# Block 1's down-projection as seven products, weight differences made ahead through ScalarE's DMA queue, and the final norms moved into the up stages

## The chip, the cores and the metric

The kernel runs on one core of a Trainium2 chip. The metric is the device time in microseconds of one execution; the time of a kernel is the median of its runs. Engines are named as in the profile: PE is TensorE, PEld its weight loads, DVE VectorE, ACT ScalarE, POOL GpSimd, SP the engine whose queue issues most DMAs.

## The reference, cut to what matters

One layer of an encoder: attention and an mLSTM mix 2048 prompt rows and 128 sample rows, then comes the part that the change touches, a gated convolutional feed-forward network with a norm on both sides (D_MODEL 1024, D_FF 2816):

```python
def conv_ffn(h, buf, w_up, w_conv, b_conv, w_down):
    S = h.shape[1]
    u = h @ w_up
    ext = jnp.concatenate([buf.astype(u.dtype), u], axis=1)
    y = b_conv
    for j in range(CONV_W):
        y = y + ext[:, j:j + S] * w_conv[j]
    gate, up = jnp.split(y, 2, axis=-1)
    out = (jax.nn.gelu(gate, approximate=True) * up) @ w_down
    return out, ext[:, S:]
...
    ffn, new_buf = conv_ffn(rms_norm(x, norm_g[2]), conv_buf, w_up, w_conv, b_conv, w_down)
    x = x + rms_norm(ffn, norm_g[3])
```

`w_down` has 2816 rows and 1024 columns. All of it is float32.

## The kernel before

**Arithmetic.** Every product is taken in three passes (`mm3`, L93 to L97): each operand is split into a high part (a cast on ScalarE, L1265) and a low part (a subtraction on VectorE, L1266, the two are `split`), and L95 multiplies high by high, L96 and L97 high by low and low by high, all into one PSUM accumulator.

**Stages.** The first 1319 us hold the projections, attention, mLSTM and `project` (the output projection with the first residual, rows `x2d`). Then the feed-forward runs over three blocks of tiles of 128 rows, `FBLOCKS`: tiles 0 to 5, 6 to 11, and 12 to 15 with the sample tile. Each block has an up stage and a down stage.

The **up stage** loops over f, 22 slices of 128 of the 2816 inner columns. The slice's u is made of seven products of half-sized matrices (`product`, accumulators `ua`, `ub`, `uec`) with weight quads `wu` of 128x512; block 0 computes sums of the weights and stores them (`wsd`), blocks 1 and 2 load them. VectorE adds the products up (L1419, L1491, L1493, L1508), the convolution `y` takes ScalarE and VectorE (L1438 to L1442), the gated product g (L1514) goes to DRAM (`gd`) through GpSimd's queue. GpSimd also copies the halo columns (L1430, L1435).

The **down stage** multiplies g by `w_down`: two halves `dh` of 512 columns, each 22 k, six tiles and three passes into six accumulators (`dn`, `dnm`). `load_down` brings weights in chunks of four k (raw quads `wdr`, split into `wdh` and `wdl`, two buffers each), `fetch` brings g back from DRAM (`gr`), `split_g` splits it into `gh` and `gl` (four buffers `w3`). At a half's end VectorE copies the accumulators out (L1340), ScalarE squares them for the norm (L1344), and GpSimd's queue stores them (`f0d`, `f1d`).

**Interleaved work.** `h2_units(b + 1, ...)` prepares the next block's operand B (norm, transposes, sums, splits), a step after most k, and `later(t, rs)` finishes rows of the block before: it loads `f0d` or `f1d` and `x2d`, multiplies by the norm's factor on VectorE (L1376), adds the residual on GpSimd (L1377) and stores to the output (L1378). Before, these run in the down stages of blocks 1 and 2, between the units of `h2_units`. Raw rows live in a pool of eleven 2 KB buffers, `quad`.

**What sets the order.** The tile framework allocates buffers from pools, puts in the semaphore waits and orders each engine's instructions by a planned timeline; operations in `tc.keep_in_program_order` keep their place relative to the program. Each engine runs its own list in order, so a waiting instruction holds back all behind it on that engine. DMAs are issued from the list of the engine that names them (`nc.sync`, `nc.scalar`, `nc.gpsimd`).

## Time and profile before

| | us |
|---|---|
| runs | 2798.23, 2791.51, 2785.69 (median 2791.51) |
| profiled execution | 2788.08, its span 2786.4, granted clock 0.998 |
| block 0: up, down stage | 324.5, 195.9 |
| block 1: up, down stage | 318.2, 194.0 |
| block 2: up stage, down stage with the end | 268.4, 166.4 |

The stage lengths are read off the timeline at the first matmul of each stage (1319.0, 1643.5, 1839.4, 2157.6, 2351.6 and 2620.0 us from the span's start). A group's row in the profile reads: line, engine, operation, output<-inputs with shapes, count | busy us, mean ns of one | idle time of the engine just before them, and what ended it. A row of the timeline reads: start, length, engine, line, operation, count, and in brackets the idle time before it with its releaser.

### The profile page before, as it was taken

Reading aid. Unit: us, or ns where it says so; the run is one execution under the profiler, and the core shown is the slowest. Engines: PE = TensorE matmul, PEld = TensorE weight load, DVE = VectorE, ACT = ScalarE, POOL = GpSimd, SP = SyncE. Lnnn points to the kernel's source line nnn. Section 1 sums busy time; section 2 is a strip of 40 time slices with the busy share of each in tenths; the row PEclk is TensorE's granted clock in tenths of the full one; section 3 lists DMA queues with packets and bytes.
Section 4 is the critical chain, followed back from the end, with each engine's and each line's share of the span. In section 5 each row is a group of like instructions: output and inputs, shape, how many; then the busy total and the mean of one; then the engine's idle time right before and its main releaser. Section 6 shows DMA issues by size and latency. Waiting matters only on the chain.

```text
span 2786.4 us, 47181 instructions
## 1 busy us (share of the span) xinstructions
PE 2724.6 (98%) x16587; PEld 2549.6 (92%) x16587; DVE 1875.3 (67%) x3447; ACT 1407.9 (51%) x2836; POOL 555.4 (20%) x1095
## 2 busy tenths in 40 slices
PE   8999999999999999999999999999999999999998
PEld 7899999998899998888999988899999878999987
DVE  5344455656456667766999986457877864888855
ACT  4345455645356666533544555345555643555543
POOL 1000010211100002344533320011111421222330
PEclk9999999999999999999999999999999999999999
DMA  5544355557555455346645455644444774555585
GB/s 183 157 121 133 103 172 160 163 156 214 166 173 149 142 170 179 111 156 220 211 167 170 160 180 179 221 140 156 154 155 140 280 260 154 171 180 176 195 311 189
DMA packets 300171, 486.05 MB, mean 174 GB/s; under 512 B 55426, under 2 KB 150622, under 8 KB 299806
## 3 DMA queue, kind: packets, MB, share of 16 engines
q1 hardware_dynamic: 242334, 378.81, 43.9%
q0 software_dynamic: 19008, 70.40, 6.5%
q10 hardware_dynamic: 38592, 33.83, 3.6%
q8 instruction: 130, 2.13, 0.3%
q14 instruction: 107, 0.88, 0.1%
HBM read 359.36 MB, written 126.70 MB: 174 GB/s over the span
## 4 chain that ended last, share of the span: by engine, by line
PE 53%; DVE 3%; DMA 2%; issue 1%; POOL 1%; ACT 1%; SPq 0%; DVEq 0%; POOLq 0%; ACTq 0%
PE uec L95 6%; PE uec L96 6%; PE uec L97 6%; PE dn L97 4%; PE dn L96 4%; PE dn L95 4%; PE ua L97 3%; PE ua L96 3%; PE ua L95 3%; PE dnm L97 2%; PE dnm L95 2%; PE dnm L96 2%; PE ub L97 1%; PE ub L96 1%; PE ub L95 1%; PE wo L97 1%
## 5 line engine op out<-in xcount | busy, mean ns | idle before, releaser
L95 PE MATMUL uec<-B,wuh 128*128 128x384 f32 (+1 forms) x720 | 235.1, 328 | 3.1 <-DVE uu L1508 2.8
L96 PE MATMUL uec<-B,wuh 128*128 128x384 f32 (+1 forms) x720 | 235.1, 327 | 0.0
L97 PE MATMUL uec<-B,wul 128*128 128x384 f32 (+1 forms) x720 | 233.7, 327 | 0.0
L1266 DVE TENSOR_TENSOR gl<-gr,gh 128x768 fp32r<-128x768 f32 (+3 forms) x141 | 119.4, 856 | 153.1 <-ACT gh L1265 152.8
L1265 ACT CAST gh<-gr 128x768 fp32r<-128x768 f32 (+3 forms) x141 | 102.1, 736 | 210.3 <-PE dn L96 186.3
L1265 ACT CAST wuh<-wu 128x512 fp32r<-128x512 f32 x255 | 141.7, 618 | 110.4 <-PE uec L96 99.9
L95 PE MATMUL dn<-wdh,gh 128*128 128x512 f32 x466 | 182.7, 392 | 3.0 <-DVE ug L1419 3.0
L96 PE MATMUL dn<-wdl,gh 128*128 128x512 f32 x466 | 183.8, 394 | 0.0
L97 PE MATMUL dn<-wdh,gl 128*128 128x512 f32 x466 | 168.2, 396 | 0.0
L1266 DVE TENSOR_TENSOR wul<-wu,wuh 128x512 fp32r<-128x512 f32 x255 | 164.8, 683 | 3.8 <-POOL uu L1430 3.8
L393 DVE CUSTOM_DVE_ANT_0 tmp<-s,nb 128x640 f32<-128x640 f32 (+4 forms) x128 | 94.3, 737 | 93.7 <-PE s L383 93.1
L95 PE MATMUL vo<-wi_h,hT 128*128 128x256 f32 x544 | 155.1, 285 | 0.6 <-DVE mt L199 0.6
L97 PE MATMUL vo<-wi_h,hT 128*128 128x256 f32 x544 | 155.6, 286 | 0.0
L96 PE MATMUL vo<-wi_l,hT 128*128 128x256 f32 x544 | 154.8, 285 | 0.0
L95 PEld LDWEIGHTS uec<-B,wuh 128*128 128x128 f32 x720 | 135.0, 188 | 5.0 <-DVE uu L1508 3.8
L96 PEld LDWEIGHTS uec<-B,wuh 128*128 128x128 f32 x720 | 135.2, 188 | 0.2
L97 PEld LDWEIGHTS uec<-B,wul 128*128 128x128 f32 x720 | 135.1, 188 | 0.0
L95 PE MATMUL qk<-hT,wi_h 128*128 128x384 f32 (+1 forms) x384 | 128.5, 335 | 6.2 <-ACT qk_st L224 5.4
L406 DVE TENSOR_TENSOR ptl<-pt,pth 128x640 fp32r<-128x640 f32 (+4 forms) x128 | 93.6, 737 | 56.8 <-ACT pth L405 55.9
L394 ACT ACTIVATE tmp<-tmp,mn 128x640 f32<-128x640 f32 (+4 forms) x128 | 97.6, 762 | 63.7 <-DVE mn L393 61.3
L96 PE MATMUL qb<-hT,wi_h 128*128 128x384 f32 (+1 forms) x384 | 127.9, 333 | 0.0
L96 PE MATMUL qk<-hT,wi_h 128*128 128x384 f32 (+1 forms) x384 | 127.6, 332 | 0.0
(417 smaller groups left out, 8992.7 us busy)
## 6 DMA issues: line engine op xcount, KB each, us to landing
wu<-in_w_up SPq DMA_DIRECT2D x220, 256.0 KB, 3.8
wu<-wsd SPq DMA_DIRECT2D x176, 256.0 KB, 3.6
wdr<-in_w_down SPq DMA_DIRECT2D x132, 256.0 KB, 5.6
gr<-gd SPq DMA_DIRECT2D x78, 384.0 KB, 3.8
wi_raw<-in_w_in SPq DMA_DIRECT2D x52, 512.0 KB, 4.0
wsd<-ws POOLq DMA_DIRECT2D x88, 256.0 KB, 3.8
gd<-g POOLq DMA_DIRECT2D x44, 384.0 KB, 2.7
kraw<-kTd SPq DMA_DIRECT2D x112, 128.0 KB, 3.3
```

The costliest lines, as they stand in the source:

```text
L95: nc.tensor.matmul(out, ah, bh, start=start, stop=False, skip_group_check=onto)
L96: nc.tensor.matmul(out, ah, bl, start=False, stop=False, skip_group_check=onto)
L97: nc.tensor.matmul(out, al, bh, start=False, stop=stop, skip_group_check=onto)
L393: nc.vector.tensor_tensor_reduce(o_, s_, b_, 1.0, 3e38, ALU.add, ALU.min, accum_out=mn)
L394: nc.scalar.activation(tmp[:, :n], tmp[:, :n], AF.Exp, bias=mn, scale=-1.0, accum_out=rsum[:, i % 4, hh:hh + 1])
L406: nc.vector.tensor_tensor(s.ptl[:, sl, qc], ptv, s.pth[:, sl, qc], op=ALU.subtract)
L1265: nc.scalar.copy(h, r)
L1266: nc.vector.tensor_tensor(l, r, h, op=ALU.subtract)
```

## The change

For block 1 (`FAST`), the down-projection is a two-by-two block product: rows 6 to 8 and 9 to 11 of the tiles, k 0 to 10 and 11 to 21, columns 0 to 511 and 512 to 1023. It is computed as seven products (`SEQUENCE`) of 11 k, three tiles and three passes each, into two PSUM sets of three accumulators in turn. Some products go on top of what a set holds (`onto`); `leave` copies a set out on ScalarE or adds it on VectorE to a kept part, and `close` stores finished tiles.

The products need sums of both operands:
- `store_a`, in block 1's up stage, makes S1 to S4 from g (four VectorE operations of 128x384 for each pair of f) and stores seven pieces for each pair. The f are taken in the order 0, 11, 1, 12, ... (`ORDERS`). g is written in place of the convolution's output.
- `folds`, in block 0's down stage, makes the differences of the weights: 44 loads of 128x512 on ScalarE's queue, 44 VectorE subtractions, 44 stores from GpSimd (`wtd`), one fold of four each per four k, all pinned in program order. `w_down` lies in DRAM in another layout for it.

`later`'s units now run in the up stages of blocks 1 and 2, one half row per f from the fourth f on (`delayed`), with buffers of a new pool `spare` (six of 2 KB) that the folds and the kept parts of block 1's down stage use too. The stores of `x2d` go out on SP's queue instead of GpSimd's, the first block's `h2_units` is paced differently (eight and six steps, one bubble more), and the program is built with `dynamic_dma_scratch_size=4096`.

```diff
+FAST = (1,)
+ORDERS = [[f for k in range(NK) for f in (k, k + NK)] if b in FAST else list(range(NF)) for b in range(3)]
...
+    spare = ctx.enter_context(tc.tile_pool(name="spare", bufs=6, reuse_waits="tile"))
...
-            nc.gpsimd.dma_start(x2d[t], xr)
+            nc.sync.dma_start(x2d[t], xr)
...
-            for i in range(6):
+            for i in range(6 if late else 8):
...
+    def folds(period, plan):
+
+        live = {}
+
+        def load(k, xs):
+            if k < NK:
+                for x in xs:
+                    live[k, x] = spare_tile(f"fold{k}_{x}")
+                    tc.keep_in_program_order(nc.scalar.dma_start(live[k, x], I["w_down"][k][:, x * 512:(x + 1) * 512]))
+
+        def combine(k):
+            a, b, c, d = [live[k, x] for x in range(4)]
+            for o, x, y in ((a, b, a), (b, c, b), (c, c, a), (d, d, c)):
+                tc.keep_in_program_order(nc.vector.tensor_tensor(o, x, y, op=ALU.subtract))
+
+        def store(k):
+            if k >= 0:
+                for x in range(4):
+                    tc.keep_in_program_order(nc.gpsimd.dma_start(wtd[k][:, x * 512:(x + 1) * 512], live.pop((k, x))))
...
+    SEQUENCE = [("A11", B11, 0, False), ("A12", B21, 1, False), ("S2", T2, 0, True), ("S1", T1, 1, False),
+                ("S3", T3, 0, True), ("S4", B22, 1, True), ("A22", T4, 0, True)]
...
     def later(t, rs):
 
         def unit(half):
-            v, x, c = quad(f"f{half}{t}"), quad(f"x{half}{t}"), half * 512
+            v, x, c = spare_tile(f"f{half}{t}"), spare_tile(f"x{half}{t}"), half * 512
...
-            nc.vector.scalar_tensor_tensor(v, v, rs, g3[:, c:c + 512], op0=ALU.mult, op1=ALU.mult)
+            tc.keep_in_program_order(
+                nc.vector.scalar_tensor_tensor(v, v, rs, g3[:, c:c + 512], op0=ALU.mult, op1=ALU.mult))
...
+    def delayed(units):
+
+        for u in units:
+            next(u)
+            yield
+            next(u)
...
+    fold = folds(4, {0: ("ab",), 1: ("cd",), 3: ("combine", "store")})
...
+        def store_a(f, gt):
+            put = lambda what, k, src: nc.gpsimd.dma_start(ad[b, what][:, k, :], src)
+            first, second = gt[:, 0:384], gt[:, 384:768]
+            if f < NK:
+                put("A11", f, first)
+                held[f] = gt
+                return
+            k = f - NK
+            gt1 = held.pop(k)
+            a11, a21, a12, a22 = gt1[:, 0:384], gt1[:, 384:768], first, second
+            s3, s1, s2, s4 = [spare_tile(f"s{x}_{b}_{k}")[:, :384] for x in (3, 1, 2, 4)]
+            for o, x, y, op in ((s3, a11, a21, ALU.subtract), (s1, a21, a22, ALU.add), (s2, a22, s3, ALU.subtract),
+                                (s4, a12, s2, ALU.subtract)):
+                nc.vector.tensor_tensor(o, x, y, op=op)
+            for what, src in (("A12", a12), ("A22", a22), ("S3", s3), ("S1", s1), ("S2", s2), ("S4", s4)):
+                put(what, k, src)
...
+        done = delayed([u for t, rs in unfinished for u in later(t, rs)])
+        unfinished = []
+        for fi, f in enumerate(ORDERS[b]):
             w = pend.pop(0)
-            ahead_of(2 * f + 2)
+            ahead_of(2 * fi + 2)
+            if fi >= 3:
+                next(done, None)
...
-        done = [u for t, rs in unfinished for u in later(t, rs)]
-        unfinished = []
-        ahead = Pipe(iter(done) if last else h2_units(b + 1, done))
+        for _ in done:
+            pass
+        ahead = Pipe(iter([]) if last else h2_units(b + 1, lead=2))
...
+            mms = [ps_mm(f"dnm{b}_{i}") for i in range(2)]
+            bigs = [ps_big(f"dn{b}_{i}") for i in range(2)]
+            sets = [[bigs[i][:, 0:512], bigs[i][:, 512:1024], mms[i]] for i in range(2)]
...
+                onto = {1: 0, 4: 3, 5: 2}
+                for j in range(3):
+                    if p in kept:
+                        nc.scalar.copy(kept[p][j], acc[j])
+                    else:
+                        x = kept[onto[p]][j]
+                        nc.vector.tensor_tensor(x, x, acc[j], op=ALU.add)
...
+            for p, (_, _, set_, onto) in enumerate(SEQUENCE):
+                for c in range(3):
+                    wh, wl = pend
+                    if c < 2:
+                        pend = load_product(b, p, c + 1)
...
+                    for k in range(4 * c, min(4 * c + 4, NK)):
+                        i = 6 * p + k // 2
+                        if k % 2 == 0:
+                            if i >= 1:
+                                split_a(i + 1)
+                                fetch_a(i + 4)
...
+                        for j in range(3):
+                            tt = slice(k % 2 * 384 + j * P, k % 2 * 384 + (j + 1) * P)
+                            mm3(sets[set_][j], ah[:, tt], al[:, tt], wh[:, wk], wl[:, wk],
+                                start=not onto and k == 0, stop=k == NK - 1, onto=onto)
+                        steps += 1
+                        if steps % 2 == 0:
+                            ahead.step()
+                leave(p)
...
+                    if b == 0:
+                        next(fold, None)
...
-    nc = bacc.Bacc("TRN2", target_bir_lowering=False, num_devices=1)
+    nc = bacc.Bacc("TRN2", target_bir_lowering=False, num_devices=1, dynamic_dma_scratch_size=4096)
```

**ScalarE in block 0's down stage**, about its sixth and seventh k. `gh` is the high part of g, `b` and `B` belong to the next block's operand, `fold` to the weight differences; in brackets stand the semaphores that the instruction waits for (DMAHW: a transfer of SP's or ScalarE's queue, DMASW: one of GpSimd's). Before:

```order
L1265 CAST gh_0_6_19870<-gr_0_6_19806 128x768 [waits DMAHW7_49,DVE_49,PE_49]
L1110 COPY b_19864<-h2T_pt_1_0_19859 128x512 [waits DMASW6_49,PE_49]
L1110 COPY b_19899<-h2T_pt_1_1_19894 128x512 [waits DMASW2_49,DMASW6_49,DMASW0_49,PE_49]
L1105 CAST B_1_19741<-b_19899 128x4x128 [waits Activation_49]
L1105 CAST B_1_19738<-t_19866 128x4x128 [waits DVE_49]
L1105 CAST B_1_19736<-t_19901 128x4x128 [waits DVE_49]
L1265 CAST gh_0_7_19911<-gr_0_7_19839 128x768 [waits DMAHW0_49,PE_49]
```

Of the change:

```order
L1309 CAST gh_0_6_19871<-gr_0_6_19800 128x768 [waits DMAHW6_49,DVE_49,PE_49]
L1176 DMA fold_2_19867<-in_w_down 128x512 [waits DMASW6_49,DVE_49]
L1176 DMA fold_3_19869<-in_w_down 128x512 [waits DMAHW7_49,DMASW7_49]
L1309 CAST gh_0_7_19897<-gr_0_7_19828 128x768 [waits DVE_49,PE_49]
L1124 COPY b_19985<-h2T_pt_1_0_19980 128x512 [waits PE_49]
L1124 COPY b_20024<-h2T_pt_1_1_20019 128x512 [waits DMASW4_49,DVE_49,PE_49]
L1119 CAST B_1_19854<-b_20024 128x4x128 [waits Activation_49]
L1119 CAST B_1_19851<-t_19987 128x4x128 [waits DVE_49]
L1176 DMA fold_0_19991<-in_w_down 128x512 [waits DMAHW3_49,DMASW0_49]
L1176 DMA fold_1_19993<-in_w_down 128x512 [waits DMAHW4_49,DMASW1_49]
L1309 CAST gh_0_8_19956<-gr_0_8_19875 128x768 [waits PE_49]
```

Pairs of fold loads now stand between the casts of g, and each waits for transfers of GpSimd's queue, where the buffers' earlier contents are stored.

**ScalarE in the middle of block 1's down stage.** `wdh` is the high part of the weights, `ah` that of the first operand, `x` a kept part of the result. Before, the second half at its k 6 to 12:

```order
L1265 CAST gh_1_6_25620<-gr_1_6_25576 128x768
L1265 CAST gh_1_7_25644<-gr_1_7_25600 128x768
L1265 CAST gh_1_8_25686<-gr_1_8_25624 128x768
L1265 CAST gh_1_9_25710<-gr_1_9_25648 128x768
L1265 CAST wdh_3_25668<-wdr_3_0_0_25670 128x512
L1265 CAST wdh_3_25668<-wdr_3_0_1_25674 128x512
L1265 CAST wdh_3_25668<-wdr_3_1_0_25678 128x512
L1265 CAST wdh_3_25668<-wdr_3_1_1_25682 128x512
L1265 CAST gh_1_10_25734<-gr_1_10_25690 128x768
```

Of the change, from the end of the fourth product into the fifth:

```order
L1309 CAST ah_22_25704<-ar_22_25581 128x768
L1309 CAST ah_23_25746<-ar_23_25616 128x384
L1309 CAST wdh_4_0_25728<-wdr_4_0_0_25730 128x512
L1309 CAST wdh_4_0_25728<-wdr_4_0_1_25734 128x512
L1309 CAST wdh_4_0_25728<-wdr_4_0_2_25738 128x512
L1309 CAST wdh_4_0_25728<-wdr_4_0_3_25742 128x512
L1309 CAST ah_24_25772<-ar_24_25671 128x768
L1309 CAST ah_25_25811<-ar_25_25708 128x768
L1681 COPY x_3_0_25787<-dn_1_24874 128x512
L1681 COPY x_3_1_25788<-dn_1_24874 128x512
L1681 COPY x_3_2_25789<-dnm_1_24872 128x512
```

Four casts of weights now come after every two casts of the first operand instead of after every four, and the copies of a finished product stand behind the next product's first casts.

**VectorE at the end of block 2's up stage.** `f` is the row of the delayed norm, `ug`, `uu` and `y` belong to f = 20 and 21, `wdl` and `gl` are low parts for the down stage. Before:

```order
L1440 SCALAR_TENSOR_TENSOR y_20_0_29432<-ug_20_29378,wcv,y_20_0_29432 128x656
L1376 SCALAR_TENSOR_TENSOR f_29659<-f_29659,drs_26094,norm_row_16236 128x512
L1514 TENSOR_TENSOR g_20_29437<-y_20_0_29432,y_20_1_29424 128x512
L1517 TENSOR_TENSOR g_20_29437<-y_20_0_29432,y_20_1_29424 128x128
L1439 SCALAR_TENSOR_TENSOR y_21_1_29590<-uu_21_29516,wcv,y_21_1_29590 128x656
L1440 SCALAR_TENSOR_TENSOR y_21_1_29590<-uu_21_29516,wcv,y_21_1_29590 128x656
L1419 TENSOR_TENSOR ug_21_29544<-x_2_21_29463,uec_21_29461 128x128
```

Of the change:

```order
L1504 SCALAR_TENSOR_TENSOR y_20_0_29861<-ug_20_29807,wcv,y_20_0_29861 128x656
L1310 TENSOR_TENSOR wdl_0_29871<-wdr_0_2_29880,wdh_0_29870 128x512
L1310 TENSOR_TENSOR wdl_0_29871<-wdr_0_3_29884,wdh_0_29870 128x512
L1632 TENSOR_TENSOR uu_21_29945<-x_2_21_29892,uec_21_29890 128x320
L1638 TENSOR_TENSOR g_20_29866<-y_20_0_29861,y_20_1_29853 128x512
L1641 TENSOR_TENSOR g_20_29866<-y_20_0_29861,y_20_1_29853 128x128
L1503 SCALAR_TENSOR_TENSOR y_21_1_30019<-uu_21_29945,wcv,y_21_1_30019 128x656
L1504 SCALAR_TENSOR_TENSOR y_21_1_30019<-uu_21_29945,wcv,y_21_1_30019 128x656
L1483 TENSOR_TENSOR ug_21_29973<-x_2_21_29892,uec_21_29890 128x128
```

The norm's operation ahead of the last sums (`ug`) is gone from this place; the weights' subtractions stand nearer to it.

164 lines of the change are left out of this document (135 added, 29 removed).

## The prediction

> **What bounds the kernel now.** I read the page's engine totals first, then the windows by stage (one row per stretch: length, then busy time and count for PE, weight loads, VectorE, ScalarE, GpSimd, then granted clock, DMA share, GB/s), then the groups by shape in the down stages, last the timeline where TensorE stops.
>
> ```profile
> span 2786.4 us, 47181 instructions
> PE 2724.6 (98%) x16587; PEld 2549.6 (92%) x16587; DVE 1875.3 (67%) x3447; ACT 1407.9 (51%) x2836; POOL 555.4 (20%) x1095
> ```
> ```profile
> GB/s 183 157 121 133 103 172 160 163 156 214 166 173 149 142 170 179 111 156 220 211 167 170 160 180 179 221 140 156 154 155 140 280 260 154 171 180 176 195 311 189
> ```
> ```profile
> 1319.00:1643.50 324.50, 320.44 (x1825) 317.10 (x1824) 303.78 (x459) 167.53 (x267) 121.98 (x193) 1.00 0.53 181
> 1643.50:1839.40 195.90, 193.81 (x865) 157.85 (x866) 110.30 (x152) 94.55 (x159) 11.46 (x30) 1.00 0.55 180
> 1839.40:2157.60 318.20, 317.91 (x1825) 317.58 (x1823) 246.19 (x366) 163.23 (x271) 57.05 (x122) 1.00 0.48 154
> 2157.60:2351.60 194.00, 193.50 (x865) 157.17 (x866) 123.09 (x165) 90.95 (x156) 45.09 (x55) 1.00 0.67 230
> 2351.60:2620.00 268.40, 268.40 (x1834) 268.36 (x1833) 232.22 (x473) 153.38 (x273) 77.81 (x207) 1.00 0.56 176
> 2270.00:2340.00 70.00, 70.00 (x306) 57.18 (x305) 24.73 (x32) 21.51 (x31) 0.00 (x0) 1.00 0.54 185
> ```
>
> The rows are: up and down of block 0, up and down of block 1, up of block 2, and a stretch of block 1's down stage with nothing else in it. TensorE is busy for 193.50 of 194.00 us in block 1's down stage and for 268.40 of 268.40 in block 2's up stage. So TensorE sets the time of each of these stages, and its work counts in full as long as the others keep up. Their reserve differs: VectorE is at 303.78/324.50 = 94% in block 0's up stage, 77% and 87% in the other two, 63% in block 1's down stage.
>
> **Part 1: 99 matmuls fewer (−23.0 us).** Before, 2 halves × 22 k × 6 tiles × 3 passes = 792 matmuls of 128x512; after, 7 products × 11 k × 3 tiles × 3 = 693. The 70.00 us stretch holds about 70/0.232 = 302 of them beside the few that overlap its edges (306 counted); between two starts the timeline further down shows 0.23 (2633.61 to 2633.84). I take 0.232 us: 99 × 0.232 = 23.0. The up stage's products are untouched, and what the seven products cost the other engines is part 2.
>
> [...]
>
> **Part 2: what the others must do in block 1's down stage, now 194 − 23 − 4 = about 167 us (+2.5, bounds 0 to 17.7).**
>
> ```profile
> L1266 DVE TENSOR_TENSOR gl<-gr,gh 128x768 fp32r<-128x768 f32 x39 | 39.4, 1010 | 53.5 <-ACT gh L1265 53.4
> L1266 DVE TENSOR_TENSOR wdl<-wdr,wdh 128x512 fp32r<-128x512 f32 x44 | 31.4, 762 | 3.3 <-ACT wdh L1265 3.3
> L1376 DVE SCALAR_TENSOR_TENSOR f<-f,drs,norm_row 128x512 f32<-128x512 f32 x12 | 10.0, 830 | 4.1 <-DMA f<-f0d 4.1
> ...
> L1266 DVE TENSOR_TENSOR gl<-gr,gh 128x384 fp32r<-128x384 f32 x6 | 3.1, 554 | 1.4 <-ACT gh L1265 1.4
> ```
> ```profile
> L1265 ACT CAST gh<-gr 128x768 fp32r<-128x768 f32 x39 | 32.5, 834 | 67.7 <-PE dn L96 61.1 <-DMA wu<-in_w_up 3.3 <-DMA wdr<-in_w_down 2.2
> L1265 ACT CAST wdh<-wdr 128x512 fp32r<-128x512 f32 x44 | 24.9, 617 | 6.8 <-DMA wdr<-in_w_down 4.0 <-PE uec L96 2.7
> ...
> L1110 ACT COPY b<-h2T_pt 128x512 f32<-128x512 f32 x8 | 4.6, 581 | 1.8 <-PE h2T_pt L1093 1.6
> ```
> ```profile
> L1377 POOL TENSOR_TENSOR f<-f,x 128x512 f32<-128x512 f32 x12 | 24.0, 2004 | 38.1 <-DVE f L1376 34.9 <-DMA wdr<-in_w_down 3.1
> ```
> ```profile
> L1266 DVE TENSOR_TENSOR gl<-gr,gh 128x768 fp32r<-128x768 f32 x39 | 37.2, 956 | 63.2 <-ACT gh L1265 63.1
> L1266 DVE TENSOR_TENSOR wdl<-wdr,wdh 128x512 fp32r<-128x512 f32 x44 | 27.8, 684 | 4.9 <-ACT wdh L1265 4.9
> ```
>
> The first three views are block 1's down stage (groups of VectorE, ScalarE, GpSimd), the last is VectorE in block 0's, where no normalisation of an earlier block runs. Weight quads rise from 44 to 77, since each product has its own B operand; the A operand falls to 35 pieces of 768 columns and 7 of 384. Without the normalisation I take block 0's durations. VectorE: 77 × 0.684 = 52.7, 35 × 0.956 = 33.5, 7 × 0.554 = 3.9, and what remains of 123.1 without gl, wdl and f of this stage, 42.3 (the next block's B operands, the stage's edges, and the copies from PSUM that nine additions replace): 132 of 167 us, 79%. ScalarE: 77 × 0.617 = 47.5, 35 × 0.834 = 29.2, 7 × 0.42 = 2.9, twelve copies from PSUM at 0.581 = 7.0, the rest 90.95 − 32.5 − 24.9 = 33.6: 120, or 72%. GpSimd keeps only its stores and small operations.
>
> Neither is full, but the lead is shorter. One A piece now lasts 18 matmuls = 4.18 us and comes with two weight quads, where a piece of g came with one. The chunk of weights is shorter too: four quads last 8.4 us, the last chunk of a product (three quads) 6.3, where four lasted 16.7. A chunk's load lands in 5.6 us (row below), its first cast and subtraction take 1.3, 6.9 in all, and two buffers stand for weights: each load has a chunk's time of lead, so only the short chunks come near. The bounds: nothing late, 0; every pair of cast and subtraction in series, 0.834 + 1.010 + 2 × (0.617 + 0.762) = 4.60 per 4.18 us, 0.42 × 42 = 17.7. The rows show the two engines overlapping at 63% and 47% (VectorE's and ScalarE's busy shares) and TensorE never idle for more than 0.5 us in all, so I stay near the lower end: six events of 0.4, +2.5. The end of a product is no wait: two PSUM sets alternate, and three evacuations (about 2 us) lie inside the next product's 23 us.
>
> **Part 3: weight differences in block 0's down stage (+2, bounds 0 to 12).** 44 loads of 256 KB on ScalarE's queue, 44 subtractions on VectorE, 44 stores from GpSimd.
>
> ```profile
> wdr<-in_w_down SPq DMA_DIRECT2D x132, 256.0 KB, 5.6
> ...
> wsd<-ws POOLq DMA_DIRECT2D x88, 256.0 KB, 3.8
> ...
> f0d<-fr POOLq DMA_DIRECT2D x17, 256.0 KB, 7.2
> ```
> ```profile
> L275 ACTq DMA_DIRECT2D vd<-va_st x32: 326/326/353, 21.3 to 672.3; - x32
> ```
> ```profile
> L1284 POOL DMA_DIRECT2D wsd<-ws x84 | 45.4, 541 | 77.2 <-DVE ws L1282 76.1 <-issue 0.4
> ```
>
> VectorE: 44 × 0.684 = 30.1, to 140 of 196 us (72%). ScalarE: 44 issues × 0.326 = 14.3, to 109 (56%). GpSimd: 44 × 0.541 = 23.8, to 35. Traffic: 88 × 0.262 MB = 23 MB in 196 us, 180 to about 298 GB/s; the page's slices at 280 and 260 (block 1's down stage begins there) and 311 show the chip doing that with TensorE busy. Hidden, all of it, under TensorE's 196 us.
>
> The uncovered part is order. A fold's third and fourth load stand in ScalarE's program between two casts of g and wait for buffers which the fold before stores. If that store is late, the next cast waits behind, then VectorE's subtraction, then TensorE. The store follows the first two subtractions (1.37), two issues (1.08) and a landing of 3.8 (like wsd) to 7.2 (like f0d): 6.3 to 9.7 us after the fold's differences begin. The next fold's third load stands two k steps, 8.4 us, later. So 0 to 1.3 us of holding, against a cast with 4.18 − 0.83 − 0.96 = 2.4 us to spare: normally nothing reaches TensorE. The upper bound is ten folds at 1.2 (half of that 2.4), 12; I take 2.
>
> [...]
>
> **Part 4: up stages take the delayed normalisation and, in block 1, the sums of A (+2 and +1.5, bounds 0 to 10.4 together).**
>
> ```profile
> 2182.59 1.82 POOL L1377 TENSOR_TENSOR f<-f,x 128x512 f32<-128x512 f32 x1 [3.14 <-DMA wdr<-in_w_down]
> ```
> ```profile
> 2183.17 2.05 DVE L1266 TENSOR_TENSOR gl<-gr,gh 128x768 fp32r<-128x768 f32 x1
> ```
> ```profile
> PE uec L95 <- DVE uu L1508: 1.4, 2, 0.8
> ```
>
> A half row costs VectorE 0.83 plus what GpSimd's addition takes from its neighbours: the subtraction that met one took 2.05 instead of 0.956, at most 1.1. So 1.9 at worst. Block 1's up stage: 246.2 + 44 × 0.554 (24) + 12 × 1.9 (23) = 293 of 318, 92%. Block 2's: 232.2 + 23 = 255 of 268, 95%. The measure is block 0's up stage (last row): at 94%, 1.4 us waited for VectorE past its first 26 us. That makes +2 for block 1, which also has 55 more stores and twelve additions and their stores on GpSimd (57 + 55 × 0.541 + 24 + 12 × 0.541 = 117 of 318), and +1.5 for block 2. The bound is rival B's.
>
> **Part 5: the end of block 2's up stage (−4.0) and what is late next (+1.5).**
>
> ```profile
> 2626.14 0.75 DVE L1376 SCALAR_TENSOR_TENSOR f<-f,drs,norm_row 128x512 f32<-128x512 f32 x1 [2.40 <-DMA f<-f0d]
> ```
> ```profile
> 2627.63 0.30 PE L97 MATMUL uec<-B,wul 128*128 128x320 f32 x1
> 2630.12 0.71 PE L95 MATMUL dn<-wdh,gh 128*128 128x512 f32 x1 [2.19 <-DVE ug L1419]
> ...
> 2633.61 0.39 PE L95 MATMUL dnm<-wdh,gh 128*128 128x512 f32 x1
> 2633.84 0.40 PE L96 MATMUL dnm<-wdl,gh 128*128 128x512 f32 x1
> ```
>
> VectorE stood 2.40 us for a load of the normalisation; behind it, the release of the accumulator came late, TensorE stood 2630.12 − 2627.93 = 2.2 us, and the next eight matmuls took until 2633.61, 3.49 us where 8 × 0.232 = 1.86 would do: 1.6 lost at half clock. With what the restart costs (the first matmul takes 0.71 instead of 0.40) about 4.0 together. After the change no such operation stands there. Of the tail's other work, unchanged, I add 1.5 because the loads of g and weights that follow now meet it 2 us earlier. The bounds are −4 (all kept) and 0 (the waits for loads come back whole).
>
> [...]
>
> The stores of x2 on SP's queue, the two extra bubbles and the smaller descriptor memory count 0: phase 1 has no operation more.
>
> **Sum.** −23.0 + 2.5 + 2 + 2 + 1.5 − 4.0 + 1.5 = −17.5. From the profiled execution's 2788.1 (span 2786.4, 1.7 around it) that is 2770.6. It lies 3.4 under the median of the runs shown, 2791.5, so a median after is 2771 to 2774: I say 2772.
>
> **Rivals.** A, block 1's down stage becomes bound by the cast and subtraction in series: its part is 17.7 instead of 2.5, 2772 + 15 = 2787. For it: 77 quads in less time, a chunk in half the time. Against: 79% and 72%. Chance 0.11.
>
> B, the up stages saturate. Block 2 has 36.2 us free, 1.65 per f, and a half row asks 1.9 in twelve f: 0.25 × 12 = 3. Block 1 has 72 us free, 3.27 per f; every second f asks 4 × 0.554 + 1.9 = 4.1, over by 0.8 in nine: 7.4. Together 10.4 against 3.5 in the sum: 2779. Against it: the f between asks only 1.9 of 3.27 and can make it up. Chance 0.15.
>
> C, slower: ScalarE stands at the fold loads. Its place is the pair of loads behind g's cast; it decides once subtractions, issues and landing together exceed the 8.4 us by more than the 2.4 to spare, that is once a store lands in more than 8.4 + 2.4 − 1.37 − 1.08 = 8.3 us instead of 3.8 to 7.2. Price per fold as at block 2's boundary: 2.2 idle and 1.6 at half clock, about 4.0; ten folds, 40 against the 2 counted: 2772 + 38 = 2810. For it: GpSimd's stores share a stage that rises to 298 GB/s, and f0d already shows 7.2. Chance 0.13.
>
> D, it doesn't do what it says: the preparation of block 2's B operands, most of the 42.3 on VectorE, outlasts the shortened stage and TensorE gets its 23 us back as a wait: 2772 + 23 − 2.5 = 2792. Against: preparation steps every second k, and it is through by about two thirds of them. Chance 0.03.
>
> **Numbers.** The forecast has 0.58, with a range of its own of 2762 to 2780. A measurement of this kernel tells about 0.5% from no change, 14 us: faster means under 2777.5. Faster: 0.95 of the forecast (0.55) and a third of B (0.05), 0.60. Slower: C and a shadow of A, 0.15. The rest, 0.25, is within. The range goes up past A and to D, not to C, and down to the sum with no stall at all (−23 − 4 = −27, 2761) less 2 for the spread between runs: 2759 to 2794.
>
> **What would show it.** Block 1's down stage near 168 us with TensorE over 97% busy: part 1 right. A ScalarE wait at the fold loads above 2 us, and TensorE gaps behind g's cast in block 0's down stage: C. TensorE in block 2's up stage waiting on VectorE's sums ten times or more: B. TensorE waiting for weight or A splits in block 1's down stage: A. The half clock near 2630 gone: part 5. The forecast is wrong if the four stages together lose more than 14 us.

## The result, and the profile after

The changed kernel takes 2776.43 us (median of 7 runs, 2773.73 to 2780.18), the kernel before 2792.08 us beside it (7 runs, 2785.69 to 2798.23): a ratio of 0.9944 with a 95% interval of 0.9931 to 0.9957, 15.7 us or 0.56% faster. The forecast was 2772 in a range of 2759 to 2794.

The page of the changed kernel, its span and its engine totals:

```profile
span 2776.4 us, 47521 instructions
PE 2704.6 (97%) x16488; PEld 2530.5 (91%) x16488; DVE 1938.4 (70%) x3563; ACT 1420.4 (51%) x2879; POOL 610.1 (22%) x1177
```

TensorE issues 16587 − 16488 = 99 matmuls fewer and is busy 20.0 us less; the span is 10.0 us shorter. The rest is the price of the other edits, and the windows by stage show where it was paid (columns as in the prediction; the rows are block 0's up and down stage, block 1's, and block 2's up stage):

```profile
1319.75:1641.70 321.95, 319.58 (x1825) 317.01 (x1824) 299.14 (x452) 166.40 (x267) 116.30 (x190) 1.00 0.54 180
1641.70:1841.80 200.10, 194.18 (x867) 157.53 (x865) 138.66 (x199) 93.85 (x158) 39.18 (x75) 1.00 0.85 289
1841.80:2162.80 321.00, 320.28 (x1837) 319.80 (x1836) 285.37 (x424) 163.75 (x274) 121.87 (x198) 1.00 0.65 205
2162.80:2335.50 172.70, 168.95 (x750) 135.24 (x750) 121.66 (x183) 106.58 (x196) 24.33 (x43) 1.00 0.74 243
2335.50:2610.20 274.70, 271.21 (x1842) 269.82 (x1841) 247.35 (x485) 154.65 (x272) 103.05 (x223) 1.00 0.66 208
```

Against the rows of before, block 1's down stage (fourth row) falls from 194.0 to 172.7 us, block 0's down stage rises from 195.9 to 200.1, and block 2's up stage from 268.4 to 274.7. In these three TensorE is no longer always busy: 5.9, 3.8 and 3.5 us of it are idle, where before it was 2.1, 0.5 and 0.0.

For comparing many kernels the stages are cut below at the first matmul of each long, unbroken run of one kind, so the 8 to 12 us in which up and down matmuls mix count to the up stage. Two profiles stand for before, two for the changed kernel (the second of each is from the experiments).

| us | before | again | changed | again |
|---|---|---|---|---|
| start to block 0 | 1319.1 | 1323.8 | 1319.7 | 1322.4 |
| block 0 up | 335.3 | 335.5 | 333.6 | 333.4 |
| block 0 down | 184.9 | 184.7 | 188.5 | 188.2 |
| block 1 up | 329.2 | 329.2 | 330.3 | 330.3 |
| block 1 down | 183.0 | 183.3 | 164.8 | 164.0 |
| block 2 up | 278.6 | 278.1 | 281.6 | 281.6 |
| block 2 down | 148.6 | 147.8 | 148.2 | 148.2 |
| last matmul to the end | 7.7 | 7.8 | 9.7 | 9.6 |
| span | 2786.4 | 2790.2 | 2776.4 | 2777.7 |

From block 0 on, a stage comes back within 0.8 us from one profile of a kernel to the next; the part ahead of it varies by several us (1318.6 to 1329.0 over all profiles here). So the stages tell what an edit does better than the total does. From block 0 to the end the changed kernel is 10.9 us shorter (1456.0 against 1466.9, means of the pairs), where the medians of the runs differ by 15.7. The other 4.8 us are in no stage that the change was meant to touch; they would have to come from the varying first part, which these profiles do not settle.

What TensorE waited for in block 1's down stage (first view) and in block 2's up stage (second), in us, times and longest (waits view of the changed kernel):

```profile
PE dn L104 <- ACT ah L1309: 2.1, 1, 2.1
PE dn L106 <- DVE al L1310: 1.1, 1, 1.1
PE h2T_pt L1107 <- DVE x2r L1099: 0.5, 1, 0.5
```
```profile
PE uec L104 <- DVE uu L1632: 1.6, 1, 1.6
PE uec L104 <- DVE x L1611: 1.2, 1, 1.2
PE uec L104 <- DVE uu L1483: 0.8, 1, 0.8
```

Block 1's down stage has one stop for a cast of A and one for a subtraction. Block 2's up stage has three stops for VectorE's sums, where before it had none.

### The profile page after: what moved, and what is told of

It reads as the page before. It is cut to its first block, busy times and chain, and to the rows that moved or that the text cites. A ratio compares the mean times of both kernels' runs of the same rounds, so it can differ in the third digit from the quotient of the medians.

```text
span 2776.4 us, 47521 instructions
## 1 busy us (share of the span) xinstructions
PE 2704.6 (97%) x16488; PEld 2530.5 (91%) x16488; DVE 1938.4 (70%) x3563; ACT 1420.4 (51%) x2879; POOL 610.1 (22%) x1177
## 3 DMA queue, kind: packets, MB, share of 16 engines
q8 instruction: 130, 2.13, 0.3%
## 4 chain that ended last, share of the span: by engine, by line
PE 53%; DVE 3%; issue 2%; DMA 2%; ACT 1%; POOL 1%; DVEq 0%; POOLq 0%; SPq 0%; ACTq 0%
PE uec L104 6%; PE uec L105 6%; PE uec L106 6%; PE dn L106 3%; PE dn L104 3%; PE dn L105 3%; PE ua L106 3%; PE ua L105 3%; PE ua L104 3%; PE dnm L106 2%; PE dnm L105 2%; PE dnm L104 2%; PE wo L106 2%; PE wo L104 2%; PE wo L105 2%
## 5 line engine op out<-in xcount | busy, mean ns | idle before, releaser
L1310 DVE TENSOR_TENSOR gl<-gr,gh 128x768 fp32r<-128x768 f32 (+3 forms) x92 | 73.9, 812 | 98.9 <-ACT gh L1309 91.1
L1309 ACT CAST gh<-gr 128x768 fp32r<-128x768 f32 (+3 forms) x92 | 65.0, 719 | 143.8 <-PE dn L105 110.3
L105 PE MATMUL qb<-hT,wi_h 128*128 128x384 f32 (+1 forms) x384 | 127.8, 333 | 0.0
L106 PE MATMUL qk<-hT,wi_l 128*128 128x384 f32 (+1 forms) x384 | 127.5, 332 | 0.0
L106 PE MATMUL qb<-hT,wi_l 128*128 128x384 f32 (+1 forms) x384 | 127.2, 331 | 0.0
L104 PE MATMUL qb<-hT,wi_h 128*128 128x384 f32 (+1 forms) x384 | 127.1, 331 | 0.0
```

The source lines that it names most:

```text
L104: nc.tensor.matmul(out, ah, bh, start=start, stop=False, skip_group_check=onto)
L105: nc.tensor.matmul(out, ah, bl, start=False, stop=False, skip_group_check=onto)
L106: nc.tensor.matmul(out, al, bh, start=False, stop=stop, skip_group_check=onto)
L1309: nc.scalar.copy(h, r)
L1310: nc.vector.tensor_tensor(l, r, h, op=ALU.subtract)
```

## The experiments

Nine kernels are the changed kernel with one or two parts undone or altered, one is a combination of three edits, and two repeat the kernels themselves. Stage lengths are those of the table's cut unless a range is given in the windows' cut; ratios are to runs of the kernel before on the same chip. A stop is the time that TensorE loses between two starts beyond the usual 0.23 us; the waits view and the brackets of the timeline give the idle time alone, which is 0.16 us less for matmuls of 128x512 (one is recorded with 0.39 us, the next starts 0.23 after it).

**The same kernels again.**

> The changed kernel once more, for a second profile. If the stalls of the first profile belong to the kernel: 2776 us, block 0's down stage again 4 to 5 us longer than before's 195.6, block 1's down stage again about 21 shorter, block 2's up stage again 5 to 8 longer than 267.2, with stops at the same instructions. If they are chance of one execution: the stops stand at other places and single stages differ by 3 us or more from the first profile.

> The kernel before once more, for a second profile. If the first profile of before is typical, its stages come back within 1 us (335 up and 185 down in block 0, 329 and 183 in block 1, 279 and 149 in block 2) and the first phase ends near 1049 us. If the first phase varies by chance, as the changed kernels' do (1051 to 1059), it ends 2 to 10 us later and the whole takes 2790 to 2797, which would explain why the medians differ by 15.7 and the two profiles by 10.0.

The changed kernel again: 2778.78 us (2775.15 to 2780.28), 0.9941 (0.9929 to 0.9954), the same stages and the same stops to 0.8 us. Before again: one run at 2791.9 us with a span of 2790.2, its stages within 0.8 us of the first profile; only the first part was 4.7 us longer. The stalls belong to the kernels. One price does not: at the end of block 2's up stage, where the first profile of before has 2.19 us of idle time and half clock behind it (a granted clock of 0.50 for 3.41 us; the second matmul is recorded with 0.63 us), the second has 1.63 us and no half clock (its second matmul takes 0.40; its timeline):

```profile
2634.61 0.47 PE L95 MATMUL dn<-wdh,gh 128*128 128x512 f32 x1 [1.63 <-DVE ug L1419]
2634.92 0.40 PE L96 MATMUL dn<-wdl,gh 128*128 128x512 f32 x1
```

**The seven products undone, everything else kept.**

```diff
-FAST = (1,)
+FAST = ()
```

> Undoes the seven products alone (FAST empty): folds, delayed norms, pools and pacing stay, the differences are stored and not read, nothing is stored by store_a. If the 99 matmuls carry the whole gain: 23 us more in block 1's down stage, less the 2 to 4 us of stalls that go with the products and their sums, so 2794 to 2799, slower than before by 2 to 7. If half of the gain came from the delayed norms: 2784 to 2788.

2800.67 us (11 runs), 1.0019 (1.0007 to 1.0030): slower than before. Block 1's down stage takes 188.1 us instead of 164.4. The products carry more than the whole gain, 2800.67 − 2778.78 = 22 us, and the other edits alone cost about 0.2% of the time. The 188.1 is 5 more than before's 183.1: in this kernel, too, the preparation of the next block is paced otherwise, and TensorE stops for 3.2 us and runs another 1.9 us short on half clock at the boundary of the two halves.

**The weight differences left out.** Block 1's products read the raw blocks.

```diff
-    fold = folds(4, {0: ("ab",), 1: ("cd",), 3: ("combine", "store")})
+    fold = iter(())
...
-            src = I["w_down"][k] if blk < 4 else wtd[k]
+            src = I["w_down"][k]
```

> Leaves out the weight differences: no loads on ScalarE's queue, no subtractions, no stores in block 0's down stage; block 1's products take the raw blocks of w_down in their place (same bytes, same matmuls, so block 1's rows of the output hold other values). If the folds cause the 4.5 us that block 0's down stage lost: that stage back at 195 to 197, 2772 us. If it is the pacing of the next block's preparation (eight steps instead of six): still 199 to 200, 2775 to 2776.

2779.64 us, 0.9950 (0.9936 to 0.9963): no change in the time. Block 0's down stage goes from 188.3 to 186.8, so 44 loads, 44 subtractions and 44 stores cost about 1.5 us there; 2.0 us of the stage's 3.5 remain without them. These are small against what the stage does by itself: in four kernels here whose edits lie elsewhere (delayed norms undone whole or in part, squares later, other buffers) it takes 187.6 to 189.1 us. In the changed kernel's list of DMA issues (count, size, median us to landing) the median lies inside the bounds that the forecast gave the stores, 3.8 to 7.2; single stores took 3.6 to 8.8:

```profile
wtd<-fold POOLq DMA_DIRECT2D x44, 256.0 KB, 6.3
```

**The pacing of the preparation, in block 0's down stage alone.**

```diff
-            for i in range(6 if late else 8):
+            for i in range(6 if b < 2 else 8):
...
-        ahead = Pipe(iter([]) if last else h2_units(b + 1, lead=2))
+        ahead = Pipe(iter([]) if last else h2_units(b + 1, lead=2 if fast else 0))
```

> Undoes one part in block 0's down stage: the preparation of block 1's operand is paced as before (no start delay, six steps between units); the folds stay. If the pacing puts the transposes on the boundary of the two halves and costs about 2 of that stage's 3.4 us: stage 186 to 187 (from 188.3), 2774 to 2776. If the folds' traffic is what delays the loads there: stage unchanged at 188 or longer, 2777 to 2779.

2778.65 us, 0.9945 (0.9932 to 0.9958), and a stage of 187.5 us. The stop for the transposes moves off the boundary of the halves, another of 1.8 us comes at 1732 us. The stage is 0.8 us shorter where about 2 were expected, no more than it varies by itself, so the pacing is not shown to cost anything.

**The delayed norms undone.** The units run between the preparation's steps again, with raw rows of `quad`.

```diff
-        done = delayed([u for t, rs in unfinished for u in later(t, rs)])
+        waiting = [u for t, rs in unfinished for u in later(t, rs)]
+        done = delayed([])
...
-        ahead = Pipe(iter([]) if last else h2_units(b + 1, lead=2))
+        ahead = Pipe(iter(waiting) if last else h2_units(b + 1, waiting, lead=2))
```

> Undoes the delayed norms alone: the units of block 0 and 1 run in the down stages of blocks 1 and 2 again, from the pool of eleven raw rows. If delaying them pays about what it costs, as forecast (4.0 gained at the boundary, 3.5 and 1.5 paid): 2776 plus 0 to 5; block 2's up stage back at 267 to 270, the stop of 2.3 us and the half clock at its end back, block 1's down stage 2 to 5 us longer. If VectorE is what stalls block 2's up stage and the norms are its last straw, with nothing lost in the down stages: 2770 to 2772.

2780.17 us, 0.9957 (0.9942 to 0.9971). Block 2's up stage is back at 277.0 us (4.6 less), and block 1's down stage takes 172.9 (8.5 more), where TensorE now waits for the weights:

```profile
PE dn L105 <- DVE wdl L1310: 5.0, 3, 2.7
PE dn L104 <- ACT wdh L1309: 2.2, 2, 1.5
```

About half of the 8.5 us is idle time (7.7 us in its waits view, 3.7 in the changed kernel's), and most of the rest are two periods of half clock (they begin at 2216.24 and 2229.90 us). This is rival A's sign, in the kernel in which the norms and the products share a stage. Its mechanism is not shown: VectorE is busy for 76% of these 180 us and ScalarE for 59%, and ahead of TensorE's stops at 2226 to 2229 us ScalarE itself stands 3.32 us for a load, so that late loads have a part in it. Delaying block 0's norms into block 1's up stage is what keeps the products fed. It costs nothing to speak of there: that stage takes 330.3 us here too, without the norms, and 329.4 with the norms and without the products. The 1.1 us that it is longer than before's 329.2 go with the sums of A.

The other half of the expectation was missed: with the norms back, block 2's down stage does not begin with a stop of 2.3 us and half clock (0.8 and 0.9 us of idle time, as in the changed kernel). The norm's operation is pinned in program order now and no longer stands ahead of the last sums.

**Only block 1's norms back in block 2's down stage.**

```diff
+        waiting = [u for t, rs in unfinished for u in later(t, rs)]
+        done = delayed([] if last else waiting)
...
+        ahead = Pipe(iter(waiting) if last else h2_units(b + 1, lead=2))
```

> Block 0's final norms stay delayed (block 1's up stage), block 1's go back to block 2's down stage. If VectorE has no room for them in block 2's up stage and some in its down stage: up stage 277 (from 281.6), down stage within 1 us of 148.2, so 2772 to 2774. If the wait for the norm's first load at the boundary comes back (2.3 us and the half clock): 2776 to 2778.

2780.14 us, 0.9955 (0.9942 to 0.9968). The up stage falls to 276.9, the down stage rises to 153.2: 4.7 gained, 5.0 lost. The loss is one stop at the boundary (3.2 us of idle time) and the half clock behind it, an estimated 1.8, what is left of the 5.0. The waits of TensorE there, and ScalarE's timeline:

```profile
PE dnm L104 <- ACT gh L1309: 4.0, 2, 3.2
PE dn L104 <- DVE ug L1483: 0.8, 1, 0.8
```
```profile
2628.34 0.72 ACT L1309 CAST gh<-gr 128x640 fp32r<-128x640 f32 x1 [3.61 <-DMA gr<-gd]
```

ScalarE stands 3.61 us for a row of g whose load shares the boundary with the norms' loads. So at that stage's start the norms cost what they save in the up stage.

**The squares of the next block's rows later, in block 1's down stage.**

```diff
-            if not late:
+            for _ in range(4 if b == 2 else 0 if late else 1):
                 yield 0.0, 0.0
...
-                nc.scalar.activation(out, x, AF.Square, accum_out=ssq)
+                sq_ = nc.scalar.activation(out, x, AF.Square, accum_out=ssq)
+                if b == 2:
+                    tc.keep_in_program_order(sq_)
```

> In block 1's down stage the squares of the x2 rows, which wait for their load at the head of ScalarE's queue, come three steps later and are pinned there; the loads keep their places. If these waits (10.8 us of ScalarE in four) cause the two stops of 2.3 and 1.5 us: both gone, block 1's down stage 161 to 162 (from 164.4), 2773 to 2775. If the short chunks of weights cause them: the stops stay at the same products, 2776 to 2779.

2781.86 us, 0.9959 (0.9947 to 0.9971), and the first stop grew from 2.3 to 3.85 us, with half clock behind it (1.7); the second (1.1 us of idle time in the waits view) is gone. The stage takes 165.2. This theory fell for the larger stop. For the smaller one it may hold, but the longer stop ahead of it also gave its loads more time. In the changed kernel's timeline (SP, VectorE, ScalarE, TensorE, between 2182 and 2192 us) the order of events is to be seen:

```profile
2183.18 4.78 SPq L1555 DMA_DIRECT2D ar<-ad_A  x3
```
```profile
2182.20 0.95 DVE L1638 TENSOR_TENSOR y<-y,y 128x768 f32<-128x768 f32 x1
```
```profile
2190.67 0.83 ACT L1309 CAST ah<-ar 128x768 fp32r<-128x768 f32 x1 [1.04 <-DMA ar<-ad_A]
```
```profile
2188.80 0.39 PE L106 MATMUL dn<-wdh,al 128*128 128x512 f32 x1
2189.03 0.39 PE L106 MATMUL dnm<-wdh,al 128*128 128x512 f32 x1
2191.55 0.50 PE L104 MATMUL dn<-wdh,ah 128*128 128x512 f32 x1 [2.13 <-ACT ah L1309]
2191.89 0.40 PE L105 MATMUL dn<-wdl,ah 128*128 128x512 f32 x1
2192.12 0.39 PE L104 MATMUL dnm<-wdh,ah 128*128 128x512 f32 x1
```

The load of the second product's first piece (`ar`, L1555) is issued when the up stage's very last g (L1638) is done, 20 us into the down stage as the windows cut it, since both use the four raw rows of one pool (`row`). SP itself stands only 0.5 us for that g; the planner has also put four loads of weights ahead of it (L1364, issued until 2182.64). Its cast starts 7.5 us after the issue, and TensorE has run dry. With the squares out of the way the same row of ScalarE reads (squares later; its lines lie two further down):

```profile
2194.38 0.83 ACT L1311 CAST ah<-ar 128x768 fp32r<-128x768 f32 x1 [6.86 <-DMA ar<-ad_A]
```

**Other buffers for those two pieces.**

```diff
-            if i < 5:
+            if i < 5 or i in (6, 7):
```

> The first two pieces of the second product's A operand (pieces 6 and 7) go into raw rows of the weight pool (quad) instead of the four rows that the up stage's last convolution still holds. If block 1's stop at the second product (2.3 us, 3.9 with the squares later) comes from the load of piece 6 waiting for these rows: its load issues 10 us or more earlier, the stop is gone, block 1's down stage 162 to 163 (from 164.4). If traffic or the wait for x2 rows at ScalarE's head causes it: the stop stays at 1.5 to 2.5 us and the stage at 164 to 165.

The loads now go out 6 us earlier (10 or more were expected), before that g,

```profile
2177.35 2.82 SPq L1552 DMA_DIRECT2D ar<-ad_A  x4
```

the stop shrinks to 0.2 us, and block 1's down stage takes 162.1 us instead of 164.4. This theory held. The time, 2775.87 us and 0.9942 (0.9930 to 0.9954), can't be told from the changed kernel's; 2 us are less than its interval.

**x2's stores back on GpSimd's queue.**

```diff
-            nc.sync.dma_start(x2d[t], xr)
+            nc.gpsimd.dma_start(x2d[t], xr)
```

> Puts the stores of x2 back on GpSimd's queue, all else as changed. If the queue is worth nothing, as forecast: the output projection stays at 267 to 270 us (first matmul of the projection to the first of block 0's up stage), time within 2 us of 2778. If moving these stores is what shortened it: back to 270 to 274, 3 to 4 us slower.

2790.55 us (12 runs), 0.9996 (0.9984 to 1.0008): with this one line back, no gain can be told any more (from block 0 to the end 2.6 of the 10.9 us are left). The projection takes 270.2 us against 267.7 and 269.4 in the changed kernel's profiles; kernels here with the stores on SP's queue take 267.1 to 270.3, so this tells nothing. The loss is far from the edit: block 0's down stage takes 198.2 us instead of 188.3. Its rows, first in the changed kernel, then with the line back (columns as before):

```profile
1653.33:1841.80 188.47, 183.75 (x817) 149.04 (x817) 128.37 (x184) 88.66 (x150) 37.48 (x71) 1.00 0.87 296
1657.06:1855.27 198.21, 188.66 (x816) 151.88 (x817) 128.93 (x184) 89.08 (x151) 35.74 (x71) 0.97 0.84 279
```

TensorE is idle for 9.55 us instead of 4.7, and the granted clock is half for 10.24 us; busy for 8.6 of them, TensorE loses about 4.3 there. The two make most of the 9.9. ScalarE's waits in the stage, in the same order:

```profile
ACT B L1095 <- DMA x2r<-x2d: 5.6, 4, 2.0
ACT gh L1309 <- DVE fold L1181: 5.4, 2, 3.3
```
```profile
ACT B L1095 <- DMA x2r<-x2d: 16.1, 5, 5.8
ACT gh L1309 <- DMA wtd<-fold: 9.9, 3, 4.9
```

Both are waits at the head of ScalarE's list: for the next block's rows (16.1 us instead of 5.6), and, as rival C has it, at the fold loads for a store that has not landed (9.9 us). Their totals alone prove little: the second profile of the changed kernel has 9.7 us for the rows and 3.4, 4.9 and 7.0 at the fold loads (for a store, a subtraction and an earlier load), and its stage takes 188.2 us. What counts is where such a wait falls. The lists show another order: on SP's list the planner now puts seven weight loads instead of three ahead of the second of these rows' loads (SP's timeline, changed kernel, then with the line back):

```profile
1653.90 1.84 SPq L1364 DMA_DIRECT2D wdr<-in_w_down  x3
1659.10 0.33 SPq L1079 DMA_DIRECT2D x2r<-x2d  x1
```
```profile
1659.06 6.15 SPq L1364 DMA_DIRECT2D wdr<-in_w_down  x7
1666.43 0.33 SPq L1079 DMA_DIRECT2D x2r<-x2d  x1
```

The row's load goes out 13 us after its partner's instead of 6, ScalarE stands for it, and TensorE has its first stop, 3.0 us and the half clock, at 1674 us. The kernel before has these stores on GpSimd's queue too, and its stage takes 184.9: the loss belongs to this order, not to the queue.

**The same without the weight differences**, to part order and folds.

```diff
-            nc.sync.dma_start(x2d[t], xr)
+            nc.gpsimd.dma_start(x2d[t], xr)
...
-    fold = folds(4, {0: ("ab",), 1: ("cd",), 3: ("combine", "store")})
+    fold = iter(())
...
-            src = I["w_down"][k] if blk < 4 else wtd[k]
+            src = I["w_down"][k]
```

> The run with x2's stores on GpSimd's queue, in which block 0's down stage took 198 us, without the weight differences (block 1's products take raw blocks of w_down, so block 1's rows of the output hold other values). If the folds make the other order dear (ScalarE held 9.9 us at fold loads, and their traffic delaying the x2 rows, 16.1 us of waits): stage back to 186 to 188, time 2778 to 2781. If the order alone does it, with the squares at ScalarE's head before their load has landed: stage 195 to 198 with the stop of 3 us at its start, time 2788 to 2791.

2789.72 us (11 runs), 0.9983 (0.9972 to 0.9993); the stage takes 192.9 us. Neither expectation was met whole: the time is that of the order alone, the stage lies between the two. Without the folds the other order costs 192.9 − 186.8 = 6.1 us. With it the folds cost 198.2 − 192.9 = 5.3 us, under the changed kernel's own order 1.5. TensorE's idle time falls from 9.55 to 6.33 us without them, and the half clock from 10.24 to 3.41. So the folds are dearer in the other order, and ScalarE's waits at their loads fit rival C's mechanism; the runs do not part them from the folds' traffic.

**Three edits together**: pieces 6 and 7 in other buffers, block 0's pacing as before, and block 1's norms in block 2's down stage, begun four steps late and with a step more between load and use.

```diff
+    def spaced(u):
+        next(u)
+        yield 0.0, 0.0
+        yield 0.0, 0.0
+        next(u)
+        yield 0.0, 1.0
...
-        ahead = Pipe(iter([]) if last else h2_units(b + 1, lead=2))
+        ahead = Pipe(iter([bubble()] * 4 + [spaced(u) for u in waiting]) if last else h2_units(b + 1, lead=2 if fast else 0))
```

> Three edits on the changed kernel: pieces 6 and 7 as in the run above; block 1's final norms in block 2's down stage, begun four steps after the boundary and with one step more between load and use; block 1's preparation paced as before. If the stalls named so far are separate: block 2's up stage 277 and its down stage 149 or less, block 1's down stage 162 to 163, block 0's 187.5, together 7 to 9 us under the changed kernel: 2768 to 2772. If VectorE's work just moves its stall with it, as with the norms split without delay (up 4.7 less, down 5.0 more): 2776 to 2779.

2770.91 us (2769.52 to 2772.63), 0.9928 (0.9916 to 0.9940). All five runs lie under the changed kernel's twelve (2773.73 to 2780.28). Block 0's down stage 186.2, block 1's 161.1, block 2's up stage 277.0 and its down stage 148.6: the stalls were separate. From block 0 to the end this version is 8.9 us shorter than the changed kernel, and its runs lie under both kernels'; the ratios' intervals of the two changed versions still overlap.

## Why the prediction was right, point by point

The direction held and so did the main term. That the median came within 4.4 us of the forecast is partly luck: in the stages themselves, from block 0 to the end, the change gained 10.9 us where 17.5 were forecast. Block 1's down stage gave 18.75 of the 20.5 forecast, and the prices were on the whole higher: block 0's down stage 3.5 (2 forecast), block 1's up stage 1.1 (2), block 2's up stage with its boundary 3.3 longer (1.0 shorter forecast), the end 1.9 (0). Block 0's up stage, which no term touches, is 1.9 shorter; why is open.

**Part 1** held. Matmuls of 128x512 follow each other at 0.23 us as before (2188.80 and 2189.03, 2191.89 and 2192.12 us in the timeline above), and block 1's down stage is shorter by 23.0 less the stalls that it gained.

**Part 2** had the size about right and the cause wrong. The stage gained 18.75 us, so 23.0 − 18.75 = 4.25 were paid instead of 2.5. They were not short chunks or casts in series (VectorE was busy 121.66 of 172.7 us, 70%, where 79% were reckoned): 2.3 were a buffer shared with the up stage's last convolution, as the run with other buffers shows, and the smaller stop (1.1 us) is gone with the squares later, which does not settle its cause. The forecast costed the loads of A as a fetch like g's before, and did not ask which buffers they land in and who releases those.

**Part 3** gave 2; block 0's down stage paid 3.5, of which the folds are about 1.5 (run without them). VectorE at 138.66 us, GpSimd at 39.18 and 289 GB/s came as reckoned (140, 35, 298). The other 2 are not settled: the run with the pacing as before gives back 0.8, no more than the stage varies between kernels.

**Part 4** gave 2 + 1.5. Block 1's up stage paid 1.1. Block 2's paid 4.6 (281.6 against 277.0 without the norms); its three stops in the waits view above make 3.6 of them. Among the terms of the sum this was mis-sized most, though the price of a half row was right. VectorE's timeline ahead of the first stop shows two of them:

```profile
2409.12 0.74 DVE L1431 SCALAR_TENSOR_TENSOR f<-f,drs,norm_row 128x512 f32<-128x512 f32 x1
2409.78 2.39 DVE L1310 TENSOR_TENSOR wul<-wu,wuh 128x512 fp32r<-128x512 f32 x2
...
2419.59 0.74 DVE L1431 SCALAR_TENSOR_TENSOR f<-f,drs,norm_row 128x512 f32<-128x512 f32 x1
2420.25 0.89 DVE L1503 SCALAR_TENSOR_TENSOR y<-uu,wcv,y 128x656 f32<-128x656 f32 x1
2421.06 1.93 DVE L1503 SCALAR_TENSOR_TENSOR y<-ug,wcv,y 128x656 f32<-128x656 f32 x1
```

Each takes 0.74 and slows what runs beside GpSimd's addition (from 2409.95 for 1.68 us and from 2420.42 for 1.88: 2.39 for two subtractions that take 1.28, 1.93 for an operation of 0.89), 1.8 us for each half row. Between 2409 and 2428 us VectorE has one pause of 0.25 us. The step that was too low was to judge by the stage's mean, 95%: an f with a half row asks VectorE for 232.2/22 + 1.8 = 12.4 us and lasts 268.4/22 = 12.2, and the reserve lies in the ten f without one. Rival B, which counted per f, had 3 us for this stage.

**Part 5** held in its sign: no half clock stands at block 2's boundary (the granted clock is 1.00 from 2617 to 2625 us), and what remains is two stops with 0.80 and 0.87 us of idle time, about 2.2 us lost with the restarts, where 4.0 were. That is −1.8 where −4.0 + 1.5 were forecast. But the 4.0 was one execution's: the second profile of before loses about 2.2 us there, without half clock, and against it nothing is gained. The changed kernel's timeline:

```profile
2618.51 0.47 PE L104 MATMUL dn<-wdh,gh 128*128 128x512 f32 x1 [0.80 <-DVE ug L1483]
2618.82 0.39 PE L105 MATMUL dn<-wdl,gh 128*128 128x512 f32 x1
```

**x2's stores at 0** was the largest miss. With all other edits in place this line decides whether the change pays: 0.9944 with the stores on SP's queue, 0.9996 without. The reckoning looked only at phase 1, where the stores stand, and there no difference can be told. It left out that the planner's timeline carries a change of one queue into the order of everything behind it.

**Rivals.** A and C did not decide in the changed kernel, but something like each was met in an experiment: A's sign with the norms in the products' stage (8.5 us), C's with the other order (5.3 us for the folds, not 40). Half of C's sign stood in the changed kernel already: ScalarE waits at the fold loads, up to 3.3 us at a time, but no stop of TensorE behind a cast of g is among those of block 0's down stage. B was there in block 2's up stage, with three waits for VectorE's sums where its sign asked for ten, and not in block 1's. D was not: TensorE had its 23 us.

The end grew by 1.9 us after the last matmul, in some kernels here and not in others (7.6 to 8.1 us without the folds, without the products, or with x2 on GpSimd's queue; 9.5 to 9.7 otherwise). Why was not settled.

## What to carry to other kernels

When work is taken off the engine that bounds the kernel, ask of each new operand not only how many transfers it needs but which buffers they land in and which late instruction releases those. Where work is moved into another stage, reckon the reserve of the very steps it lands in, not the stage's mean, and keep it off the boundaries, where here ScalarE stood 3.61 us for a load: the same norms stopped the up stage, stopped the down stage's start, and cost 0.4 us from its fifth step on. Where a planner sets the order, measure also the edits that look like nothing: here one queue name was worth as much as the whole measured gain.

## What was not expected of the hardware

The length of a stop alone does not tell whether the half clock follows. In the timeline of the second product above TensorE is idle for 2.13 us, and the matmuls go on at 0.23 us (2191.89, 2192.12). In the run with x2 on GpSimd's queue and no folds it was idle for 1.94 us, and the matmuls after it came 0.42 us apart (its timeline):

```profile
1682.76 1.70 PE L1107 MATMUL h2T_pt<-ident,x2r 128*128 128x128 f32 x8 [1.94 <-DVE x2r L1099]
1684.11 0.78 PE L104 MATMUL dnm<-wdh,gh 128*128 128x512 f32 x1
1684.69 0.63 PE L105 MATMUL dnm<-wdl,gh 128*128 128x512 f32 x1
1685.11 0.63 PE L104 MATMUL dnm<-wdh,gh 128*128 128x512 f32 x1
```

The granted clock in the traces tells more. In the changed kernel's trace it falls to 0.50 three times between 17 and 2770 us, at 108.38, 408.75 and 712.54, each time for 3.41 us; the three begin 300.37 and 303.79 us apart, 88 and 89 times 3.4133. In the 3.41 us ahead of each, at a clock of 1.00, TensorE is busy for 1.12, 1.42 and 1.36 us. Below are three pairs of neighbouring stretches of this length (columns as before): the end of block 2's up stage in the kernel before, the stop of 1.94 us, and the stop of 2.13 us in the changed kernel. The first two are cut where the half clock begins, the last 432 and 433 times 3.4133 us after 712.54.

```profile
2626.76:2630.17 3.41, 1.23 (x10) 0.99 (x8) 3.38 (x9) 2.25 (x5) 0.79 (x3) 1.00 0.25 99
2630.17:2633.58 3.41, 3.41 (x8) 2.68 (x9) 3.41 (x7) 2.49 (x5) 0.46 (x1) 0.50 0.67 186
```
```profile
1679.67:1683.08 3.41, 1.47 (x8) 0.90 (x8) 2.27 (x3) 3.41 (x8) 0.75 (x2) 1.00 0.67 227
1683.08:1686.49 3.41, 3.41 (x14) 2.93 (x12) 3.41 (x6) 2.83 (x5) 0.00 (x0) 0.50 0.40 113
```
```profile
2187.10:2190.51 3.41, 2.32 (x10) 1.58 (x9) 3.41 (x7) 2.53 (x5) 2.25 (x4) 1.00 1.00 383
2190.51:2193.92 3.41, 2.37 (x10) 1.83 (x11) 2.99 (x4) 2.82 (x5) 0.00 (x0) 1.00 0.98 347
```

In the first two pairs TensorE is busy for 1.23 and 1.47 of 3.41 us, and the next stretch runs at half clock. The stop of 2.13 us falls across the cut between its two stretches: it leaves 2.32 and 2.37 us of work in them, and the clock stays at 1.00. What sets the clock these few cases do not show, nor what follows a stretch with between 1.47 and 2.32 us of work.
